# Attention's PSUM copies with the scheduler's rank of 60 instructions earlier

## The chip, the cores and the metric

One core of a Trainium2 chip runs the whole kernel. The metric is the device time of one execution in microseconds (us). The engines are named as in the profile: PE is TensorE (its matmuls; PEld its weight loads), DVE is VectorE, ACT is ScalarE, POOL is GpSimd, and SP is the queue that issues the DMAs. Matmuls write to PSUM, which has eight banks of 128 x 512 float32 words.

## The reference

One layer of a decoder trunk over 1024 tokens of width 1024: three token mixers side by side, a gated merge, an output projection and an MLP.

```
u = rms_norm(h, g_mix);  z = u @ w_in            # columns for all branches
y_nsa = nsa_mixer(q, k_c, v_c, k_s, v_s, k_w, v_w, gates)   # sparse attention
y_rnn = gelu(g_rnn) * rg_lru(causal_conv(x_rnn))            # recurrence
y_x   = cross_attention(q_x, mem) @ w_xo
h = h + (sum_b sigmoid(gate_b) * y_b) @ w_o
h = h + relu(rms_norm(h) @ w_up)**2 @ w_down;  out = rms_norm(h, g_final)
```

The sparse attention has 16 heads in 4 groups that share keys and values. For each block of 128 queries it adds three softmax attentions with their gates: over 63 compressed keys, over the 8 selected blocks of 64 keys (top-k of the compressed scores), and over a window of 512 keys.

## The kernel before

Every float32 product is made of float32r parts: an operand is split into a high part (a copy rounded by ACT) and a low part (the difference, by DVE), and `mm3` adds high x high, high x low and low x high in one PSUM bank. Transposed probabilities are split in the same way.

The program runs in stages. First the input is normalised and turned, the compressed keys and the first projections are made. Then comes the stage that matters here: cross attention and the sparse attention, with everything else that they don't need woven in between. After it come the output projection and the MLP.

Sparse attention walks over 4 groups g and 8 query blocks i, 32 units in all. `scores` makes the compressed scores, their softmax and, from the fifth block on, the top-k mask (`im`, `m`, `rp`, lines 741 to 760, on DVE and POOL). Then four pieces follow per unit (window and selected keys, two pairs of heads each). `sub_in` makes the scores of a piece in pss banks; the eviction at line 822 (DVE) adds the mask, writes E or Ew and takes the maximum; ACT makes the exponential (826); DVE and ACT scale by one over the sum and the gate (836 to 839). `sub_out` and `cmp_out` turn these probabilities: PE transposes four 128 x 128 blocks into a pst bank, `split_p` copies the bank to ph (ACT, 644) and the rest to pw (DVE, 645), and products with V add ph and pw into the unit's pso bank. `done` copies the finished pso to parts (ACT, 871) and stores it. PSUM has 2 banks for psg (projections), 2 for pst, 3 for pss and 1 for pso.

The woven work (`fill`) is a list of generators: projections of the groups, gates, the eight recurrences (`rnn_main`, r0 to r7) and merges. A `Weave` takes steps of `fill` so that they keep to 1.5 times PE's columns in attention. `rnn_main` has on ACT the Tanh and Exp of lines 938 to 940, Sqrt (944), Square (952) and on DVE the scan (951) and what follows.

What the program writes down is not the order in which engines run. Tile's scheduler goes over all instructions with a plan of its own of how long each takes, and whenever an engine is free in the plan it takes, among the instructions that are ready, that with the earliest rank; the rank is the place in the program. So the order on each engine is fixed when the program is built; on the chip each engine runs its list in that order, and semaphores hold what is not ready.

Of the kernel before, what the change touches and what calls it, by code (L numbers as in the profile page):

```python
# [12 lines left out]
AF = mybir.ActivationFunctionType  # L13
OP = mybir.AluOpType
# [32 lines left out]
HELD = 1  # L47
MIX = 1.5
LAG = 1


def seq(gens):
    for g in gens:
        yield from g
# [81 lines left out]
def body(tc, A, out):  # L136
    nc = tc.nc
    act, dve, pool, pe = nc.scalar, nc.vector, nc.gpsimd, TensorQueue(tc)
    dma = nc.sync.dma_start

    with ExitStack() as top:
# [97 lines left out]
        def load_split(src, shape, pl=w4, bufs=2, raw=None):  # L239
            if raw is None:  # L240
                raw = load_raw(src, shape, pl, bufs)
            hi = pl.tile(shape, F32R, name="whi", tag="whi", bufs=bufs)
            lo = pl.tile(shape, F32R, name="wlo", tag="wlo", bufs=bufs)
            if lo_engine[0] is pool and shape[1] == KC:
                act.activation(hi, raw, AF.Copy)  # L245
                for x in (slice(0, KC // 2), slice(KC // 2, KC)):
                    pool.tensor_tensor(lo[:, x], raw[:, x], hi[:, x], OP.subtract)  # L247
            else:
                split(hi, lo, raw, lo_eng=lo_engine[0])
            return hi, lo  # L250

        psum = top.enter_context(tc.tile_pool(name="psum", bufs=1, space=PSUM))
        with ExitStack() as mid:
# [50 lines left out]
            def z_weights(ci):  # L304
                return A["wz"][ci], [P, KC, P]
# [17 lines left out]
            with tc.tile_pool(name="e0", bufs=1) as e0:  # L323
# [55 lines left out]
                for ch in range(2):  # L379
                    zt = rw("zkv")  # L380
                    w = load_split(*z_weights(KV_CHUNK + 2 + ch))
# [259 lines left out]
            def split_p(pt, rows, w):  # L641
                ph = ap.tile([P, 512], F32R, name="ph", tag="ph", bufs=PB)
                pw = ap.tile([P, 512], F32R, name="pw", tag="pw", bufs=PB)
                act.activation(ph[:rows, :w], pt[:rows, :w], AF.Copy)  # L644
                dve.tensor_tensor(pw[:rows, :w], pt[:rows, :w], ph[:rows, :w], OP.subtract)  # L645
                return ph, pw

            def fold_out(po):
# [193 lines left out]
            def attention():  # L842
                queue = []

                def beside(a):
                    b = queue.pop(0) if len(queue) > LAG else iter(())
                    live = True
                    for _ in a:
                        yield
                        if live:  # L850
                            live = next(b, 0) is None
                            yield
                    for _ in b:
                        yield

                for g in range(G):
                    yield "wait", f"group{g}"
                    KV = [None, None]
                    for i in range(NQ):
                        nb, wb = i + 1, min(i + 1, 5)  # L860
                        ts = slice(i * P, (i + 1) * P)
                        q = load_q(q_hi[g, 0:4, :, ts].rearrange("h d t -> d h t"),
                                   q_lo[g, 0:4, :, ts].rearrange("h d t -> d h t"))
                        gts = gates[:, i, g * 12:(g + 1) * 12].rearrange("p (h b) -> p h b", b=3)
                        unit = {}
                        cS, sel_mask = scores(g, i, q, gts)
                        yield

                        def done(unit=unit, ts=ts, g=g):
                            t = ap.tile([P, 512], F32, name="parts", tag="fold", bufs=1)  # L870
                            act.activation(t, unit["po"], AF.Copy)
                            for y, part in zip(yn_d, (t[0:64], t[64:128])):
                                dma(y[2 * g:2 * g + 2].rearrange("c (e d) t -> d (c e) t", d=HD)[:, :, ts],
                                    part.rearrange("d (h q) -> d h q", q=P))
                        unit["done"] = done
                        for si, (br, p) in enumerate([(1, 0), (1, 1), (0, 0), (0, 1)]):
                            if i == 0 and p == 0:
                                KV[br] = load_kv(q_hi[g, 4 + br], q_lo[g, 4 + br], v_d[br, g], [P, S])
                            k0, n, mask = ((0, nb, sel_mask), (i + 1 - wb, wb, wmask[:, 640 - wb * P:]))[br]
                            Es = []  # L880
                            yield from beside(sub_in(Es, q, KV[br][:2], k0, n, mask, i, p, br, gts))
                            out_ = sub_out(unit, Es, KV[br][2], k0, n, p, si == 3)
                            queue.append(seq([cmp_out(unit, g, cS, 8 * nb), out_]) if si == 0 else out_)
                    if g:
                        yield "done", f"attn{g - 1}"
# [196 lines left out]
            def spare(name):  # L1082
                return fx.tile([P, 512], F32, name=name, tag="e", bufs=2)
# [185 lines left out]
            for j in range(NQ - 2):  # L1269
# [7 lines left out]
                if j == 0:  # L1277
                    for c in (6, 7):
                        t = spare("gm1")
# [8 lines left out]
            rows = [out_rows(NQ - 2)]  # L1288
# [122 lines left out]
            while n < len(dsteps):  # L1411
# [34 lines left out]
                for j in range(4):  # L1446
# [10 lines left out]
                    elif s == 2:  # L1457
                        t = h_half(j, 0)
                        dve.tensor_tensor(t, ps, t, OP.add)
                        dma(h_d[j][:, 0:512], t)  # L1460
                    elif s == 5:
                        v = keep_["v", j] = piece("dv")
                        dve.tensor_tensor(v, ps, keep_["u2", j], OP.add)
                        t = h_half(4 + j, 1)
                        pool.tensor_tensor(v, v, t, OP.add)
                        t = h_half(j, 1)
# [140 lines left out]
```

## Time and profile before

| | |
|---|---|
| median of 3 runs | 2135.46 us (2135.0 to 2138.74) |
| profiled execution | 2138.6 us |
| its span, first to last instruction | 2136.8 us |
| PE busy | 2000.6 us (94%) |
| DVE, ACT, POOL busy | 1463.2, 1135.0, 631.6 us |
| granted clock of PE, mean | 0.977 |

Busy time alone does not say what ends a stage. PE is the busiest engine throughout; where it stands idle, the row of its next instruction names what ended the wait. A granted clock of 1.00 is 2.4 GHz, 0.50 is 1.2 GHz.

### The profile page before, as it was taken

To read this page: it belongs to the slowest core of one execution; us is meant where nothing else is said; L and a number is where in the kernel's file an instruction comes from. 1 tells how busy PE (TensorE), PEld (TensorE's weight loads), DVE (VectorE), ACT (ScalarE), POOL (GpSimd) and SP (SyncE) were. 2 spreads that over 40 slices of the span, in tenths; PEclk is the share of its full clock that TensorE was granted. 3 is DMA by queue.
4 is the path that set the end of the run, shared out by engine and by line. 5 is a ranking of instruction groups with operands and counts; after the bars stand their busy time and mean duration, and the time that the engine had idled before them with its cause. 6 is when DMAs were issued, how large, how long until landed. Compare 5 with 4: busy or idle time off the path is not lost.

```text
span 2136.8 us, 30179 instructions
## 1 busy us (share of the span) xinstructions
PE 2000.6 (94%) x10276; PEld 1670.9 (78%) x10276; DVE 1463.2 (68%) x3211; ACT 1135.0 (53%) x2234; POOL 631.6 (30%) x573
## 2 busy tenths in 40 slices
PE   7988989999998999899999998999899999999997
PEld 6777868888877887777778787878688887888776
DVE  5344376776777777577877867855767777796564
ACT  5333367677667675585776756643322222444353
POOL 0010111242422433133432322311667774010210
PEclk9999999999999999999999999999999999999999
DMA  5655335311431212423123343453344446944433
GB/s 200 176 184 166 99 108 152 121 46 56 107 118 40 61 50 75 132 76 123 51 60 99 127 134 105 152 187 111 128 158 157 147 154 207 331 137 143 143 94 123
DMA packets 160578, 269.37 MB, mean 126 GB/s; under 512 B 19368, under 2 KB 71336, under 8 KB 160424
## 3 DMA queue, kind: packets, MB, share of 16 engines
q1 hardware_dynamic: 160424, 267.44, 40.5%
q8 instruction: 81, 1.33, 0.3%
q14 instruction: 73, 0.60, 0.1%
HBM read 180.87 MB, written 86.51 MB: 125 GB/s over the span
## 4 chain that ended last, share of the span: by engine, by line
PE 60%; DVE 15%; DMA 8%; ACT 6%; issue 6%; POOL 4%; SPq 1%; POOLq 0%; DVEq 0%; ACTq 0%
PE psg L80 29%; PE pss L80 16%; PE pst L80 6%; PE pso L80 5%; PE pst L84 4%; DVE pw L645 2%; DVE W L951 1%; DVE Ew L822 1%; DMA yn<-yn_d 1%; DMA q_hi<-W 1%; DMA wraw<-in_wz 1%; DVE sx L837 1%; DVE E L822 1%; DMA X<-kv_d 1%; DMA q_lo<-W 1%
## 5 line engine op out<-in xcount | busy, mean ns | idle before, releaser
L80 PE MATMUL psg<-uh,whi 128*128 128x512 f32 x928 | 383.3, 413 | 8.9 <-DVE qxl L225 6.2
L80 PE MATMUL psg<-uh,wlo 128*128 128x512 f32 x928 | 371.1, 400 | 0.5 <-DVE wlo L225 0.5
L80 PE MATMUL psg<-ul,whi 128*128 128x512 f32 x928 | 371.1, 400 | 0.0
L645 DVE TENSOR_TENSOR pw<-pst,ph 128x512 fp32r<-128x512 f32 (+1 forms) x352 | 217.4, 622 | 74.6 <-ACT ph L644 73.5
L644 ACT ACTIVATE ph<-pst 128x512 fp32r<-128x512 f32 (+1 forms) x352 | 187.3, 538 | 93.8 <-PE pst L84 92.5
L80 PEld LDWEIGHTS psg<-uh,wlo 128*128 128x128 f32 x928 | 177.8, 192 | 39.2 <-DVE wlo L225 0.9
L80 PEld LDWEIGHTS psg<-uh,whi 128*128 128x128 f32 x928 | 178.1, 192 | 37.2 <-DVE qxl L225 6.4
L80 PEld LDWEIGHTS psg<-ul,whi 128*128 128x128 f32 x928 | 178.4, 192 | 24.6 <-issue 0.4
L247 POOL TENSOR_TENSOR wlo<-wraw,whi 128x512 fp32r<-128x512 f32 x98 | 130.9, 1355 | 183.4 <-ACT whi L245 183.4
L80 PE MATMUL pss<-KA,Q 128*128 128x320 f32 (+5 forms) x416 | 145.0, 352 | 9.0 <-DVE sx L822 3.7
L80 PE MATMUL pso<-ph,V 128*128 128x256 f32 (+1 forms) x544 | 130.5, 305 | 8.1 <-DVE fold L652 6.1
L80 PE MATMUL pss<-KB,Q 128*128 128x320 f32 (+5 forms) x416 | 135.2, 329 | 0.0
L826 ACT ACTIVATE E<-E,sx 128x128 f32<-128x128 f32 (+7 forms) x128 | 98.8, 772 | 51.1 <-DVE sx L822 50.5
L80 PE MATMUL pso<-pw,V 128*128 128x256 f32 (+1 forms) x544 | 123.9, 294 | 0.0
L826 ACT ACTIVATE Ew<-Ew,sx 128x640 f32<-128x640 f32 (+4 forms) x128 | 88.5, 691 | 66.3 <-DVE sx L822 65.9
L84 PE MATMUL pst<-ident,E 128*128 128x128 f32 x576 | 95.3, 281 | 22.3 <-DVE pw L645 15.4
L80 PEld LDWEIGHTS pso<-ph,V 128*128 128x128 f32 x544 | 96.5, 193 | 23.0 <-DVE fold L652 6.4
L225 DVE TENSOR_TENSOR df<-araw,df 128x512 fp32r<-128x512 f32 x112 | 81.0, 728 | 47.7 <-ACT df L224 47.5
L80 PE MATMUL pss<-df 128*128 128x512 f32 x432 | 106.2, 389 | 0.7 <-ACT df L224 0.7
L224 ACT ACTIVATE df<-araw 128x512 fp32r<-128x512 f32 x112 | 69.1, 620 | 68.2 <-DMA araw<-act_d 29.3
L80 PE MATMUL psg<-df 128*128 128x512 f32 x384 | 99.0, 391 | 4.3 <-ACT df L224 3.2
L84 PEld LDWEIGHTS pst<-ident,E 128*128 128x128 f32 x576 | 71.9, 144 | 36.3 <-issue 21.6
(409 smaller groups left out, 5011.4 us busy)
## 6 DMA issues: line engine op xcount, KB each, us to landing
wraw<-in_wz SPq DMA_DIRECT2D x58, 512.0 KB
araw<-act_d SPq DMA_DIRECT2D x112, 256.0 KB
act_d<-as SPq DMA_DIRECT2D x64, 256.0 KB
act_d<-sq SPq DMA_DIRECT2D x48, 256.0 KB
yn_d<-parts SPq DMA_DIRECT2D x64, 128.0 KB
ura<-in_w_up SPq DMA_DIRECT2D x16, 512.0 KB
urb<-in_w_up SPq DMA_DIRECT2D x16, 512.0 KB
wdu<-in_w_down SPq DMA_DIRECT2D x32, 256.0 KB
```

Of the source, the lines that this page charges most:

```text
L80: self.tc.nc.tensor.matmul(out, w, x, start=start, stop=stop, skip_group_check=more)
L84: self.tc.nc.tensor.transpose(out, x, ident)
L224: act.activation(hi, src, AF.Copy)
L225: (lo_eng or dve).tensor_tensor(lo, src, hi, OP.subtract)
L247: pool.tensor_tensor(lo[:, x], raw[:, x], hi[:, x], OP.subtract)
L644: act.activation(ph[:rows, :w], pt[:rows, :w], AF.Copy)
L645: dve.tensor_tensor(pw[:rows, :w], pt[:rows, :w], ph[:rows, :w], OP.subtract)
L822: dve.tensor_tensor_reduce(E[:, c0:c0 + cw], ps[:, :cw], mask[:, c0:c0 + cw], -0.125, init, OP.add, OP.min, acc)
L826: act.activation(E[:, :nw], E[:, :nw], AF.Exp, bias=sx[:, hh:hh + 1], scale=-1.0, accum_out=sx[:, 2 + hh:3 + hh])
L837: dve.tensor_tensor(sx[:, 4:6], sx[:, 4:6], gts[:, 2 * p:2 * p + 2, 1 + br], OP.mult)
L951: dve.tensor_tensor_scan(gi[:, cs], r[:, cs], gi[:, cs], init, OP.mult, OP.add)
```

## The change

`tc.high_priority(60)` around an instruction gives it the rank of an instruction 60 places up in the program. The change puts it around ph and pw of `split_p` (cross attention's calls too) and around the copy to parts of `done`. Instructions, tiles and banks stay the same.

```diff
+AHEAD_OF_FILL = 60
...
             def split_p(pt, rows, w):
                 ph = ap.tile([P, 512], F32R, name="ph", tag="ph", bufs=PB)
                 pw = ap.tile([P, 512], F32R, name="pw", tag="pw", bufs=PB)
-                act.activation(ph[:rows, :w], pt[:rows, :w], AF.Copy)
-                dve.tensor_tensor(pw[:rows, :w], pt[:rows, :w], ph[:rows, :w], OP.subtract)
+                with tc.high_priority(AHEAD_OF_FILL):
+                    act.activation(ph[:rows, :w], pt[:rows, :w], AF.Copy)
+                    dve.tensor_tensor(pw[:rows, :w], pt[:rows, :w], ph[:rows, :w], OP.subtract)
                 return ph, pw
...
                             t = ap.tile([P, 512], F32, name="parts", tag="fold", bufs=1)
-                            act.activation(t, unit["po"], AF.Copy)
+                            with tc.high_priority(AHEAD_OF_FILL):
+                                act.activation(t, unit["po"], AF.Copy)
```

The order on the engines changes with it. The three pieces below are from one place, the first recurrence inside attention (about 445 to 460 us of the trace before). The numbers in the names tell tiles apart; lines of the changed program stand one to three further down (645 is 647, 822 is 824, 951 is 954).

DVE before: pst_4575 is the bank whose pw_4581 PE waits for, L951 the scan of the recurrence, L822 the score evictions (ISA; the second of each pair reads the minimum out).

```order
L822 ISA E_4570,sx_4569<-pss_4595,smask_4358,sx_4569 128x384
L822 ISA sx_4569 128x1
L645 TENSOR_TENSOR pw_4548<-pst_4544,ph_4547 128x256
L822 ISA E_4604,sx_4569<-pss_4605,smask_4358 128x384
L822 ISA sx_4569 128x1
L966 SCALAR_TENSOR_TENSOR gx_4412<-gx_4412,ysrc_4561 128x512
L822 ISA E_4604,sx_4569<-pss_4628,smask_4358,sx_4569 128x384
L822 ISA sx_4569 128x1
L951 SCALAR_TENSOR_TENSOR W3_3989<-W2_3988,W3_3989 128x512
L645 TENSOR_TENSOR pw_4581<-pst_4575,ph_4580 48x512
L953 TENSOR_SCALAR W1_3987<-W1_3987 128x512
L951 SCALAR_TENSOR_TENSOR W3_3989<-W2_3988,W3_3989 128x512
```

DVE after, around the same pw:

```order
L840 TENSOR_SCALAR Ew_4470<-Ew_4470,sx_4469 128x640
L647 TENSOR_TENSOR pw_4581<-pst_4575,ph_4580 48x512
L824 ISA E_4570,sx_4569<-pss_4595,smask_4358,sx_4569 128x384
L824 ISA sx_4569 128x1
L944 SCALAR_TENSOR_TENSOR tau_4537<-a2_4536,tau_4537 128x512
L824 ISA E_4604,sx_4569<-pss_4605,smask_4358 128x384
L824 ISA sx_4569 128x1
L969 SCALAR_TENSOR_TENSOR gx_4412<-gx_4412,ysrc_4561 128x512
L824 ISA E_4604,sx_4569<-pss_4628,smask_4358,sx_4569 128x384
L824 ISA sx_4569 128x1
L647 TENSOR_TENSOR pw_4625<-pst_4619,ph_4624 128x512
L954 SCALAR_TENSOR_TENSOR W3_3989<-W2_3988,W3_3989 128x512
```

pw_4581 stood behind the three evictions and the first scan; now it stands ahead of all of them. pw_4625, which stood two places behind the last row shown, is now ahead of both scans.

ACT before, in the same place: tau L944 are the Sqrt, W1 L952 a Square, E L826 exponentials.

```order
L944 ACTIVATE tau_4506<-tau_4506 128x512
L944 ACTIVATE tau_4537<-tau_4537 128x512
L644 ACTIVATE ph_4580<-pst_4575 48x512
L952 ACTIVATE W1_3987<-W0_3986 128x512
L826 ACT_TABLE_LOAD
L826 ACTIVATE E_4570,sx_4569<-E_4570,sx_4569 128x768
L952 ACTIVATE W1_3987<-W0_3986 128x512
L644 ACTIVATE ph_4624<-pst_4619 128x512
L826 ACTIVATE E_4604,sx_4569<-E_4604,sx_4569 128x768
```

ACT after:

```order
L646 ACTIVATE ph_4580<-pst_4575 48x512
L841 ACTIVATE Ew_4493<-Ew_4493,sx_4469 128x640
L942 ACTIVATE a2_4536<-W2_3988,cn2_574 128x512
L968 ACTIVATE gx_4412<-psg_4420 128x512
L943 ACTIVATE W2_3988<-W2_3988,cn_573 128x512
L947 ACT_TABLE_LOAD
L947 ACTIVATE tau_4506<-tau_4506 128x512
L646 ACTIVATE ph_4624<-pst_4619 128x512
L947 ACTIVATE tau_4537<-tau_4537 128x512
L955 ACTIVATE W1_3987<-W0_3986 128x512
L874 ACTIVATE parts_4648<-pso_4206 128x512
L646 ACTIVATE ph_4657<-pst_4652 128x512
```

ph_4580 stood behind both Sqrt and their table load and is now ahead of them; ph_4624 stood behind two Squares and an exponential, and is now between the Sqrt; the copy to parts of pso_4206 is ahead of the exponentials.

PE before, from the last product of the unit with bank pso_4206 on: pst_4652 are the next transposes, psg a projection of the woven work.

```order
L80 MATMUL pso_4206<-ph_4547,V_2973 128x256
L80 MATMUL pso_4206<-pw_4548,V_2973 128x256
L80 MATMUL psg_4584<-uh_99,whi_4190 128x512
L80 MATMUL psg_4584<-ul_101,whi_4190 128x512
L80 MATMUL psg_4584<-uh_99,wlo_4191 128x512
L84 MATMUL pst_4652<-ident_66,Ew_4362 128x128
L84 MATMUL pst_4652<-ident_66,Ew_4398 128x128
L84 MATMUL pst_4652<-ident_66,Ew_4362 128x128
L84 MATMUL pst_4652<-ident_66,Ew_4398 128x128
L80 MATMUL psg_4584<-uh_99,whi_4190 128x512
L80 MATMUL psg_4584<-ul_101,whi_4190 128x512
L80 MATMUL psg_4584<-uh_99,wlo_4191 128x512
```

PE after:

```order
L81 MATMUL pso_4206<-ph_4547,V_2973 128x256
L81 MATMUL pso_4206<-pw_4548,V_2973 128x256
L85 MATMUL pst_4652<-ident_66,Ew_4362 128x128
L85 MATMUL pst_4652<-ident_66,Ew_4398 128x128
L85 MATMUL pst_4652<-ident_66,Ew_4362 128x128
L85 MATMUL pst_4652<-ident_66,Ew_4398 128x128
L81 MATMUL psg_4584<-uh_99,whi_4190 128x512
L81 MATMUL psg_4584<-ul_101,whi_4190 128x512
L81 MATMUL psg_4584<-uh_99,wlo_4191 128x512
L81 MATMUL psg_4584<-uh_99,whi_4190 128x512
L81 MATMUL pso_4661<-ph_4580,VC_576 128x512
L81 MATMUL pso_4661<-pw_4581,VC_576 128x512
```

The transposes stand three products earlier, and the first products of the next unit, into pso_4661, follow the last of pso_4206 after four transposes and four projection products; before, they came only after 29 others.

## Rows read from the trace of the kernel before

**Rows 1.** The table of engines: busy time, share of the span, instructions.

```profile
PE 2000.6 (94%) x10276; PEld 1670.9 (78%) x10276; DVE 1463.2 (68%) x3211; ACT 1135.0 (53%) x2234; POOL 631.6 (30%) x573
```

**Rows 2.** Stretches: start:end, length, busy time by engine (instructions), PEclk, DMA share, GB/s.

```profile
295.00:1417.00 1122.00, 1048.98 (x5742) 880.68 (x5741) 822.85 (x2221) 740.08 (x1480) 351.94 (x380) 0.97 0.33 99
1417.00:2136.80 719.80, 691.92 (x3035) 567.19 (x3033) 494.05 (x691) 262.54 (x492) 250.99 (x164) 0.99 0.48 156
```

**Rows 3.** Waits of PE from 295 to 1417: us in total, times, longest us.

```profile
PE pst L84 <- DVE pw L645: 33.4, 26, 3.4
PE pso L80 <- ACT parts L871: 7.9, 6, 2.4
...
PE pst L84 <- DVE m L752: 5.6, 1, 5.6
PE pss L80 <- DVE sx L822: 3.7, 5, 1.5
...
PE pso L80 <- ACT ph L644: 2.0, 1, 2.0
```

**Rows 4.** Groups by line, 295 to 1417: busy us, mean ns; idle before, its releasers.

```profile
L645 DVE TENSOR_TENSOR pw<-pst,ph 128x512 fp32r<-128x512 f32 (+3 forms) x342 | 211.0, 620 | 74.3 <-ACT ph L644 73.2
L644 ACT ACTIVATE ph<-pst 128x512 fp32r<-128x512 f32 (+1 forms) x340 | 180.8, 536 | 93.1 <-PE pst L84 92.0 <-PE pso L80 0.2
...
L871 ACT ACTIVATE parts<-pso 128x512 f32<-128x512 f32 x32 | 18.7, 586 | 1.7 <-PE pso L80 1.7
```

**Rows 5.** Timeline of DVE near 454: start us, us, instruction, [idle before <-releaser].

```profile
451.86 2.28 DVE L951 TENSOR_TENSOR_SCAN W<-W,W 128x512 f32<-128x512 f32 x1 [0.84 <-POOL W L946]
454.06 0.66 DVE L645 TENSOR_TENSOR pw<-pst,ph 48x512 fp32r<-48x512 f32 x1
```

**Rows 6.** Timeline of ACT in the same place.

```profile
448.52 1.28 ACT L944 ACT_TABLE_LOAD   x1
449.82 1.16 ACT L944 ACTIVATE tau<-tau 128x512 f32<-128x512 f32 x2
450.88 0.57 ACT L644 ACTIVATE ph<-pst 48x512 fp32r<-48x512 f32 x1
```

**Rows 7.** Timeline of PE in the same place.

```profile
452.03 0.40 PE L80 MATMUL psg<-ul,whi 128*128 128x512 f32 x1
452.27 0.40 PE L80 MATMUL psg<-uh,wlo 128*128 128x512 f32 x1
454.87 1.09 PE L84 MATMUL pst<-ident,Ew 128*128 128x128 f32 x4 [2.20 <-DVE pw L645]
```

**Rows 8.** Timeline of DVE near 805.

```profile
803.82 1.27 DVE L749 SCALAR_TENSOR_TENSOR im<-hs,im 128x15 f32<-128x15 f32 x1
805.13 1.19 DVE L750 TENSOR_TENSOR im<-im,c_keep 128x16 f32<-128x16 f32 x1
...
807.47 0.68 DVE L645 TENSOR_TENSOR pw<-pst,ph 128x512 fp32r<-128x512 f32 x1
```

**Rows 9.** Timelines of PE near 808 and 874, and of ACT near 873.

```profile
808.30 0.41 PE L84 MATMUL pst<-ident,E 128*128 128x128 f32 x2 [3.39 <-DVE pw L645]
...
874.62 0.79 PE L80 MATMUL pso<-ph,VC 8*128 8x512 f32 x1 [2.39 <-ACT parts L871]
...
873.20 0.60 ACT L894 ACTIVATE W<-psg 128x512 f32<-128x512 f32 x1 [4.49 <-DMA q_hi<-W]
```

**Rows 10.** Stretches around two of the waits, columns as in rows 2.

```profile
454.80:458.20 3.40, 3.33 (x10) 2.88 (x11) 3.40 (x4) 2.28 (x6) 2.71 (x2) 0.50 0.00 0
458.20:461.60 3.40, 3.40 (x18) 2.68 (x17) 2.07 (x8) 1.44 (x3) 1.35 (x2) 1.00 0.32 77
...
1284.20:1291.00 6.80, 4.26 (x19) 4.24 (x20) 6.76 (x24) 3.64 (x7) 1.93 (x2) 0.50 0.31 97
```

**Rows 11.** A wait of DVE from 295 to 1417, and the stretch 1300 to 1375.

```profile
DVE pw L645 <- ACT ph L644: 73.2, 84, 4.7
...
1300.00:1375.00 75.00, 70.89 (x448) 61.63 (x446) 66.69 (x188) 56.58 (x102) 24.61 (x24) 0.95 0.35 107
```

## The prediction

> **What bounds the kernel now.** The table of engines comes first [rows 1]: PE is busy 94% of the span, DVE 68%, ACT 53%. So the time is PE's work plus what PE waits. The table of stretches says where a change to attention's copies can act [rows 2]: attention, with the other work woven into it, runs from about 295 to 1417 us. In those 1122.0 us PE is busy 1048.98, so it stands idle 73.0 us, and its mean granted clock is 0.97. Compared row by row, the two programs issue in the same order on PE before 295 us and behind 1417 us; only about 1,250 of PE's 10,276 instructions, all inside, have another place. I therefore leave the 295 us ahead and the 719.8 us behind as they are.
>
> The waits of PE in that stretch are next [rows 3]. 33.4 us in 26 waits end with a pw: the four transposes of a group want a pst bank, there are two, and the bank is free only when ACT has copied it (ph) and DVE has written the low part (pw). 7.9 us in 6 waits end with the copy of pso to parts (one bank), 2.0 us in 1 with a ph. One more, 5.6 us, is put down to a MAX8, but a pw ends just beside it and PE starts transposes: I count it as a pw wait. Together 48.9 us: the change can give back no more of PE's idle time than this. ph takes 0.54 us, pw 0.62, the copy to parts 0.59 [rows 4], so a bank could be empty some 1.2 us after its last transpose; longer is queueing.
>
> One such wait in full. At 454.87 PE starts transposes after 2.20 us of idleness [rows 7]. The pw it waited for ran at 454.06; ahead of it on DVE stood the scan of the recurrence (L951), for which DVE first sat idle 0.84 us (POOL) and which then took 2.28 us [rows 5]. The ph of that pw ended at 451.45, in that idle time, and had itself stood behind two Sqrt of the recurrence and their table load of 1.28 us [rows 6]. The same happens once in each of the eight recurrences (r0 to r7), at 454.9, 538.1, 694.2, 777.9, 937.5, 1025.4, 1109.5 and 1200.4 us, with 1.6 to 2.6 us of PE lost each time.
>
> **The change, part by part.** No instruction is added or taken away; ph, pw and parts get another rank, and the scheduler then orders all engines anew. On DVE 181 pw and on ACT 165 ph and 22 copies to parts now have an earlier place. The sum, against the span of 2136.8 us:
>
> *Eight recurrence waits.* In each the scan, and on ACT the Sqrt or the Square behind which the ph stood, are now behind (the order of the first is in the section on the change). What is left ahead of pw is its ph. I take the waits as gone: 8 x 2.1 us = -17 us. Bounds: 0 (another instruction takes the scan's place) to -18.
>
> *The other pw waits.* 39.0 - 17 = 22 us. I went through each in the timelines of ACT and DVE and took out what the new order puts behind. Where that is a scaling of E (L838), a gate product (L837) or a sum of the merge (L994), the wait goes: -9 us over some twenty waits, most under 1 us each. Where it is the top-k chain (L747 to L750), it stays: at 808.30 PE waited 3.39 us [rows 9] while pw stood behind rows of 1.27 and 1.19 us [rows 8], and these are still ahead of it. At the wait of 5.6 us part of the chain moves behind: -3. Together -12, bounds 0 to -22.
>
> *pso.* The one ph wait goes: -2. Of the copies to parts some move: -2 of 7.9. The largest, 2.39 us at 874.62, stays: the copy stands there behind ACT's L894, which had waited 4.49 us for a store [rows 9], and this row is still ahead. Bounds 0 to -10.
>
> *Clock.* After such a wait PE's clock can fall: in the 3.4 us behind the wait at 454.87 the granted clock is 0.50, the 1.2 GHz level, and 1.00 again in the next 3.4 [rows 10]; over 1284.2 to 1291.0 it is 0.50 as well, around the 5.6 us wait [rows 10]. A mean of 0.97 over the stretch [rows 2] is some 67 us at 0.50, in thirteen dips, six of them behind waits that I take as gone or halved. 3.4 us at half speed costs 1.7 us: six cost some 10. I take -6, since new waits will start dips of their own. Bounds +5 to -12.
>
> *Tighter packing, against the gain.* With its banks free earlier in its own plan, the scheduler pulls PE's next transposes and products forward. Walking PE's order and counting 0.23 us for a 512-column product (start to start, [rows 7]), 13 more bank reuses of pst (31, from 18 of 340) have under 2 us of PE work between the last transpose and the next. For pso it is 27 of 34, from 18: in seven units the cover was 2.9 to 7.2 us and is now 0.6 to 1.9 (the third piece of order shows one: four 512-column products and four transposes). A copy to parts costs 0.59 us plus what ACT is doing. In these seven, ACT still had 2 to 4 us ahead of it, so each can cost PE 0 to 3 us; I take 1.1: +8. For pst 13 x 0.25 = +3. Bounds 0 to +27.
>
> *What is pushed back.* The score evictions (L822) empty pss. 125 of 384 now stand behind one or two pw more, about 1 us. PE waits on them 3.7 us in 5 waits now [rows 3], and most have several us of slack. I take +6: bounds 0 to +20. It is likeliest between 1300 and 1375 us, where DVE is busy 66.69 of 75.00 us [rows 11]. The recurrence steps pushed back feed no PE instruction soon, and the stores of parts that move on SP do so by a few places, with the DMA engines at a share of 0.33 [rows 2]: nothing for either.
>
> Sum: -17 - 12 - 4 - 6 + 11 + 6 = **-22 us**, a span of 2114.8. The profiled execution took 2138.6, 1.8 more than its span and 3.1 more than the median of the runs, 2135.5. Since all the terms are differences, I take them off the median: **2113.5 us**.
>
> On a rule that speaks against the change: DVE sits idle 73.2 us in 84 waits at the head of its queue for a ph [rows 11], and in the 0.84 us before the scan [rows 5] it did not run a pw that was ready behind it. The Trainium skill (PSUM — Partial Sum Buffer, section "Engine vs sequencer instructions") says that the queues of ScalarE and VectorE are strict FIFO; the trace agrees with those 0.84 us. By that rule a pw raised to the head before its ph is done holds everything behind it, which is the second rival below; by it the sum would be that rival's +14.
>
> **The rivals.** *The waits come back (same).* The scheduler's plan fills the freed time by packing PE tighter, so pst and pso waits only change place. For it: the counts above, and that PE's waits of today already come from a plan that thought the bank free. Against it: in the recurrences the queueing of 3 us and more on DVE and ACT really leaves the path, and PE's order is unchanged or moved by a few products around half of them. Price: packing at its bound, +27, and the pushed-back work, +6, against -39: -6; with half of the -12 of the other waits not had either, 0. That is 2129 to 2136.
>
> *Blocked heads (slower).* A raised pw waits at the head of DVE for its ph, and the score evictions and scalings behind it go late; PE then waits for pss or for E. Place: 1300 to 1375, and each recurrence. Against it: DVE is idle 299 of the 1122 us [rows 2], and most evictions have slack. For it: 125 evictions moved. If one in three costs PE its 1 us, that is +42 in place of +6, so +14 in all: 2149.5 us. It decides from about 28 us of new PE waits on L822 and E.
>
> *More than forecast.* No new waits and the clock restored: -17 - 12 - 4 - 10 = -43, and up to -59 with all 48.9 us of [rows 3]: 2077 to 2098.
>
> *The rank does nothing.* Excluded, since the orders differ; it would be 2135.5.
>
> **How the numbers follow.** Forecast (2098 to 2128) 0.62; waits come back 0.17; slower 0.10; more than forecast 0.11. The range is 2093 to 2137: it leaves out the slower case and most of the best. About 0.2%, 4.3 us, is what a measurement of this kernel can tell from no change. Faster (under 2131.2): 0.62 + 0.11 and a small part of the second case, 0.76. Same: 0.14. Slower: 0.10.
>
> **What would show it.** Right: PE's waits for pw fall from 33.4 us to under 15, and none stands at a scan; the stretch from 295 takes about 1100 us in place of 1122; PE's work and both ends stay as they are. Tighter packing: PE's waits for parts stay near 8 us or grow to 15. Pushed back: PE's waits for L822 rise from 3.7 to some 10. The forecast is wrong if PE's idle time in the stretch is not under 65 us, or if waits on L822 or E take over the 33 us.

## The result and the profile after

The change makes the kernel a little slower: 2149.31 us in the median of 13 executions (2140.60 to 2157.14) against 2138.74 of 13 of the kernel before beside them, a ratio of 1.0055 with an interval of 1.0039 to 1.0070, some 11 us. The forecast was 2113.5 us, 22 us faster, with 2093 to 2137 as its range. A second set (run e15_change_again, the same program) gave 1.0065 (1.0046 to 1.0084).

The first profile fell on the slowest of the 13 executions (2157.14 us, span 2155.4). I therefore read it together with the profile of e15, whose span is 2145.3 us. The mean granted clock differs as well: 0.973 in the first profile, 0.979 in e15's, 0.977 in that of the kernel before. Over the 124 executions of the kernel before that were timed beside e1 to e17 (clock 0.974 to 0.980), an execution is on average about 1.1 us longer for each 0.001 of clock that it lacks. By this estimate e15's span is some 2 us shorter than it would be at 0.977, and the first profile's some 4 us longer. Busy time hardly moved from [rows 1]; this is the engine line of the first profile of after:

```profile
PE 2008.9 (93%) x10276; PEld 1680.0 (78%) x10276; DVE 1469.2 (68%) x3211; ACT 1136.1 (53%) x2234; POOL 638.3 (30%) x573
```

Where the time went is seen when the stretches are cut where PE issues the same instruction in both kernels. Below is the table of stretches of the kernel before, then of e15. The first three stretches are attention up to its last units, the fourth is the handover from attention's last products to the output projection, and what is left is the same work in both. First the limits and the length, then busy time per engine with counts, the clock, the DMA share.

```profile
294.50:1032.30 737.80, 689.51 (x3752) 577.61 (x3751) 534.51 (x1470) 491.50 (x998) 232.91 (x257) 0.97 0.30 89
1032.30:1222.00 189.70, 180.85 (x1001) 151.12 (x1000) 145.98 (x385) 134.93 (x273) 65.46 (x69) 0.99 0.29 86
1222.00:1358.30 136.30, 126.97 (x752) 109.15 (x751) 102.41 (x309) 84.48 (x161) 39.84 (x46) 0.97 0.36 113
1358.30:1429.20 70.90, 64.34 (x301) 53.17 (x300) 45.80 (x74) 33.18 (x63) 13.72 (x9) 0.90 0.63 204
```

```profile
295.50:1022.90 727.40, 683.97 (x3752) 574.59 (x3751) 533.16 (x1467) 490.62 (x999) 235.07 (x255) 0.98 0.31 91
1022.90:1220.40 197.50, 183.26 (x1001) 153.56 (x1000) 150.53 (x388) 136.30 (x272) 68.72 (x73) 0.97 0.28 82
1220.40:1356.80 136.40, 128.04 (x751) 110.09 (x750) 96.88 (x303) 81.35 (x157) 34.08 (x43) 0.97 0.34 105
1356.80:1439.00 82.20, 67.12 (x303) 55.38 (x302) 51.05 (x77) 36.59 (x68) 20.20 (x11) 0.90 0.59 189
```

The first 740 us gain 10.4 us (3.4 in the first profile of after), the next 190 lose 7.8, the third is unchanged: over the three, attention is 2.5 us shorter in e15 and 4.9 longer in the first profile of after. The handover then takes 82.2 us in place of 70.9, which is 11.3 us, about the whole loss. The first profile says the same (197.6 us for the second stretch, 83.3 for the handover).

The gain and the loss inside attention are in more than one profile. Cut at the same counts of PE instructions, the first stretch takes 724.9 to 734.4 us and the second 197.2 to 199.2 in the nine profiles of kernels that raise all three copies there by 60 (the two above, e1, e6, e9, e10, e13, e16, e17); in the four that keep the old order there (before, e2, e11, e12) they take 733.7 to 740.2 and 187.2 to 189.7. By the means, raised copies gain some 8 us in the first stretch and lose some 10 in the second.

Inside attention the eight waits at the recurrences are almost all gone. The waits of PE in the first profile of after, up to the handover (us in total, times, longest), answer to [rows 3]:

```profile
PE pst L85 <- DVE pw L647: 16.9, 13, 4.7
PE pso L81 <- ACT parts L874: 14.1, 7, 3.8
...
PE pss L81 <- DVE sx L824: 5.3, 6, 1.4
PE pst L85 <- DVE rp L755: 4.9, 1, 4.9
PE pst L85 <- POOL cS L738: 4.3, 5, 1.8
PE pst L85 <- DVE E L840: 3.6, 1, 3.6
```

Up to the handover the pw waits fell from 32.4 us (of the 33.4 in [rows 3]) to 16.9 (14.6 in e15), and of the eight waits at the recurrences, 16.4 us together, 0.4 us is left at the fourth (777.76 us, behind its second scan). At the first, DVE now runs the pw of 48 rows, which stood behind the scan [rows 5], 5.5 us ahead of it, and the next pw ahead of it too; PE shows no wait from 448 to 458 us:

```profile
447.41 0.68 DVE L647 TENSOR_TENSOR pw<-pst,ph 48x512 fp32r<-48x512 f32 x1
...
452.02 0.69 DVE L647 TENSOR_TENSOR pw<-pst,ph 128x512 fp32r<-128x512 f32 x1 [0.27 <-ACT ph L646]
452.92 2.30 DVE L954 TENSOR_TENSOR_SCAN W<-W,W 128x512 f32<-128x512 f32 x1 [0.20 <-POOL W L949]
```

But parts rose from 7.9 to 14.1 us, L824 from 3.7 to 5.3, and an E and more cS came in (the rp is a wait for a pw under another name, see the section on the prediction).

### The profile page after: what moved, and what is told of

The parts are those of the page before. It is cut to its first block, busy times and chain, and to the rows that moved or that the text cites. A ratio compares the mean times of both kernels' runs of the same rounds, so it can differ in the third digit from the quotient of the medians.

```text
span 2155.4 us, 30139 instructions
## 1 busy us (share of the span) xinstructions
PE 2008.9 (93%) x10276; PEld 1680.0 (78%) x10276; DVE 1469.2 (68%) x3211; ACT 1136.1 (53%) x2234; POOL 638.3 (30%) x573
## 5 line engine op out<-in xcount | busy, mean ns | idle before, releaser
L647 DVE TENSOR_TENSOR pw<-pst,ph 128x512 fp32r<-128x512 f32 (+1 forms) x352 | 217.3, 624 | 87.5 <-ACT ph L646 85.8
```

## Experiments: where the change costs

The working theory, A: the loss lies at the handover, and inside attention gain and loss cancel. Rival B: it is spread over attention, and the handover is chance. The copies are raised only up to the last two query blocks of the last group (e1, the diff below), or only in them (e2, the same with `>=`):

```diff
+            raised = [True]
...
+                with (tc.high_priority(AHEAD_OF_FILL) if raised[0] else nullcontext()):
...
+                        raised[0] = (g, i) < (G - 1, NQ - 2)
```

> ph, pw and parts keep their raised rank except in the last two query blocks of the last group, so the order of all engines at the handover from attention to the output projection is that of the kernel before. Theory A (the loss of 10.6 us lies at the handover: the profile of the changed kernel is 4.7 us late when attention ends and 17 to 21 us late just behind it): 2132 to 2141 us, and PE's waits between 295 and 1360 us as in the changed kernel. Theory B (the loss lies inside attention, by waits on parts and on pushed-back scalings): 2146 to 2152 us.

Measured: 1.0001 (0.9991 to 1.0012).

> The raised rank stands in the last two query blocks of the last group alone; the order before about 1310 us is that of the kernel before. Theory A: 2144 to 2152 us, with the loss behind 1360 us. Theory B: 2136 to 2140 us, the time of the kernel before.

Measured: 1.0044 (1.0028 to 1.0060). So nearly the whole loss comes from the copies of two of the 32 units, and raising all the others is worth nothing. The profiles agree: the handover takes 71.4 us in e1 and 79.7 in e2. A holds, B falls.

Next, which copies: only ph and pw, or only the copy to parts.

> Only ph and pw are raised, the copy to parts has its old rank. Theory C (the raised copy to parts is what costs: it pulls the next unit's first products on PE and the stores on SP forward, and the merges' loads stand behind these stores): 2120 to 2135 us, PE's waits on parts at 8 us or less, SP's waits for parts near 35 us in place of 54. Theory D (what costs is ph and pw pushing score evictions and scalings back): 2145 to 2152 us.

Measured: 1.0036 (1.0021 to 1.0050), a median of 2143.65 us, which lies between the two expectations and nearer to D's.

> Only the copy to parts is raised. Theory C: 2145 to 2152 us, the eight waits behind the recurrences' scans still there and PE's waits on parts over 12 us. Theory D: 2134 to 2139 us.

Measured: 1.0006 (0.9992 to 1.0019). It is ph and pw that cost; raising parts alone is neutral, as D said. Where the 7 us of e3 go is open: in its one profile the handover takes only 72.6 us.

## Experiments: why attention gains nothing

Theory F: the eight scan waits were worth their 17 us, and the new order of PE that raised copies bring gave it back. Rival G: a cure of the scan waits is used up by the next thing that is late. The test cures the scan waits without raising a copy:

```diff
+BEHIND = 60
...
+                        with tc.high_priority(-BEHIND):
                             act.activation(tau, tau, AF.Sqrt)
...
+                        with tc.high_priority(-BEHIND):
                             dve.tensor_tensor_scan(gi[:, cs], r[:, cs], ...)
                             act.activation(t[:, cs], gr[:, cs], AF.Square)
```

> No copy is raised; instead the recurrence's two Sqrt, two scans and two Squares get the rank of an instruction 60 places down. The pw that stood behind a scan is now ahead of it in all eight recurrences, as with the change, but only some 360 PE instructions have another place (with the copies raised in the same part: 990). Theory F (the eight scan waits were worth their 17 us; what gave it back in attention was the new order of PE that raised copies bring, with its waits on parts, E and L822): ratio 0.992 to 0.996, and waits on parts stay near 8 us. Rival G (any cure of the scan waits is used up by the next thing that is late, since DVE and ACT have the same work to do in the same time): ratio 0.998 to 1.002, the scan waits gone and other waits grown by about as much.

Measured: 1.0043 (1.0028 to 1.0057): F falls, and the kernel is even slower than G said. Of the 16.4 us that PE waited for a pw at the scans 5.4 are left, in five waits for a pw that has a scan among the six DVE instructions ahead of it (0.4 us in one with the change). Yet PE's waits up to the handover are longer than before:

```profile
PE pst L85 <- DVE pw L646: 34.0, 24, 5.4
PE pso L81 <- ACT parts L872: 13.5, 8, 2.9
PE pss L81 <- DVE sx L823: 5.8, 6, 1.5
```

Before, the same three rows were 32.4, 7.9 and 3.7 us. The kernel's loss is here: attention's three stretches take 1074.1 us against 1063.8, the handover 70.5 against 70.9. Where one wait went is seen 17 us behind the first recurrence. First DVE, then PE, of the same run:

```profile
469.87 0.69 DVE L961 SCALAR_TENSOR_TENSOR W<-W,W 128x512 f32<-128x512 f32 x1 [3.94 <-ACT W L960]
470.48 0.68 DVE L646 TENSOR_TENSOR pw<-pst,ph 128x512 fp32r<-128x512 f32 x1
```

```profile
471.22 1.06 PE L85 MATMUL pst<-ident,E 128*128 128x128 f32 x4 [3.29 <-DVE pw L646]
```

The later step of the same recurrence (L961, which needs ACT's Tanh of L960, itself later now) sits at the head of DVE's queue for 3.94 us, and a pw stands behind it. Before, PE lost nothing there. In this one place the recurrence was moved and took its wait along.

With the copies raised, the 17 us go another way. The stretch from 1022.9 us, in which e15 loses 7.8 us, is as long in every kernel that raises all three copies there (see above). Its two largest waits, ACT and PE first, then DVE and PE (e15):

```profile
1112.69 1.15 ACT L828 ACTIVATE E<-E,sx 128x1024 f32<-128x1024 f32 x1 [0.89 <-DVE sx L824]
...
1113.84 0.58 ACT L874 ACTIVATE parts<-pso 128x512 f32<-128x512 f32 x1
```

```profile
1114.46 0.51 PE L81 MATMUL pso<-ph,VC 64*128 64x512 f32 x1 [3.82 <-ACT parts L874]
```

```profile
1206.53 1.23 DVE L839 TENSOR_TENSOR sx<-sx,gates 128x2 f32<-128x2 f32 x1
1207.68 0.41 DVE L647 TENSOR_TENSOR pw<-pst,ph 128x256 fp32r<-128x256 f32 x1
1208.01 0.41 DVE L840 TENSOR_SCALAR E<-E,sx 128x384 f32<-128x384 f32 x1
```

```profile
1208.57 1.08 PE L85 MATMUL pst<-ident,E 128*128 128x128 f32 x4 [3.60 <-DVE E L840]
```

In the first, the copy to parts stands on ACT behind an exponential that waits for an eviction, and PE, pulled forward, has no products left to cover it. In the second, the scaling of E that PE needs comes behind two raised pw (0.68 us at 1205.57 and 0.41 at 1207.68) and a gate product of 1.23 us between them, whose median is 0.16 in 128. What may have made it long is in the last section.

Two more offsets and parts of the change:

> The change with 200 places in place of 60. Inside attention it raises more; at the handover its order differs (late gate products woven in from 54 products earlier, 24 products ahead of the first row's transposes, the merges' loads ahead of the last stores of parts). Theory A2: no loss at the handover, ratio 0.997 to 1.003. Rival H: the copies are raised all the more, ratio 1.004 or above. If waits inside attention grow with the offset, the pw waits fall below 22 us and those on parts, E and L822 rise above 26 us.

Measured: 1.0039 (1.0026 to 1.0051); pw waits fell further, to 14.6 us up to the handover, but parts stand at 14.2 and cS and E at 7.2 and 4.6. In its profile attention's three stretches take 1061.9 us, against 1063.8 before, and the handover 76.3: the ratio is outside A2's range (A2 is put to the test below) and just under what its rival H named.

> Only ph (ACT) is raised by 60, pw and parts keep their rank. The handover is nearly as before (12 products ahead of the first row's transposes). Theory I (inside attention raised pw block DVE's queue while they wait for ph): DVE's idle time for ph, 73 us before and 86 with the change, stays at 73 or falls, and the ratio is 0.995 to 0.999. Rival F/G (it is PE's repacking): parts waits grow to 12 us or more, ratio 0.999 to 1.003.

Measured: 1.0022 (1.0009 to 1.0034). With pw at its old rank nothing is gained either, and parts take 18.5 us, as the rival said. But DVE's idle time for ph did not go back to 73 us: it is 80.9. So what that idle time costs is not tested by this run. (The edit is the `with` around ph alone.)

## Experiments: what costs at the handover

In e15 PE waits at the handover are these, and before (1358.3 to 1429.2 us) those below:

```profile
PE pss L85 <- DVE xres L1134: 5.1, 1, 5.1
PE pst L85 <- DVE pw L647: 4.8, 2, 2.8
PE psg L81 <- ACT gm L1060: 4.3, 1, 4.3
```

```profile
PE pss L84 <- DVE xres L1131: 2.5, 1, 2.5
PE pso L80 <- ACT ph L644: 2.0, 1, 2.0
PE psg L80 <- ACT yh L224: 1.2, 2, 1.0
PE pst L84 <- DVE pw L645: 0.9, 1, 0.9
```

A2 looked at PE: the late gate products were no longer woven among the last transposes.

```diff
+LATE = 200
...
+                    with tc.high_priority(LATE):
                         for _ in z_half(late[c - 6], hf, use):
                             pass
```

> The change in full, and besides the late gate products (the eight half gates behind attention) get the rank of an instruction 200 places up. They are then woven among attention's last transposes again, until behind the last product of attention, and 24 products of the second output row stand ahead of the first row's transposes (6 with the change alone, 12 before). Theory A2 (the loss at the handover is that PE has no other work while the last pst banks are emptied, and starts the first output row's transposes too early): most of the 9 us come back, ratio 0.997 to 1.002. Rival H (the loss at the handover is on DVE, ACT and SP, where raised copies push the merges and the splits of the output rows behind): ratio stays 1.003 to 1.006.

Measured: 1.0050 (1.0035 to 1.0066). With PE's order mended nothing came back (the handover takes 79.1 us); the wait stands in one piece ahead of the first row's products:

```profile
PE psg L82 <- ACT yh L226: 11.4, 1, 11.4
```

A2 falls, and what is late is what the row needs.

That is a chain over DRAM: a unit's parts are stored, the merge loads them (L993 to L996, L1048 to L1050), DVE merges, the result is stored and loaded as a row of y (yr, L1111), split into yh and yl, and multiplied. All these transfers go through SP's one queue. SP in e15, then before (only rows on one merge, on the copies, and on a late merge's load):

```profile
1350.06 1.25 SPq L876 DMA_DIRECT2D yn_d<-parts  x2
1351.41 0.55 SPq L993 DMA_DIRECT2D yn<-yn_d  x1
1360.42 0.33 SPq L1048 DMA_DIRECT2D ymerge<-yn_d  x1
...
1365.80 0.38 SPq L994 DMA_DIRECT2D yn<-yn_d  x1
1366.22 0.43 SPq L995 DMA_DIRECT2D tn<-tn_d  x1
```

```profile
1348.77 0.32 SPq L990 DMA_DIRECT2D yn<-yn_d  x1
1351.21 0.32 SPq L992 DMA_DIRECT2D tn<-tn_d  x1
...
1353.19 0.43 SPq L991 DMA_DIRECT2D yn<-yn_d  x1
1353.71 1.24 SPq L873 DMA_DIRECT2D yn_d<-parts  x2
```

The same three loads of one merge are done at 1353 us before and at 1366 in e15: the store of parts stands ahead of them now, and a load of the late merge (L1048), also ahead of two of them, waits for PE. These are the two largest rows of SP's waits in e15 from 1320 to 1430 us:

```profile
SPq L876 <- ACT parts L874: 32.7, 2, 20.0
SPq L1048 <- PE pso L81: 8.4, 1, 8.4
```

e2 shows that this is not the whole: there the three loads are done at 1351 us, ahead of attention's end as before, and the handover still takes 79.7 us. What e15 and e2 share are late loads of the rows: the second row's last load (yr) is issued 48 us behind the end of attention before, 61 in e15 and 55 in e2. That is no proof, since these loads also wait for what comes ahead of them.

In e15 the merge stands on DVE among the raised pw of the last transposes. DVE and PE in e15 (gm itself had waited 2.99 us for a load of ymerge):

```profile
1369.65 1.20 DVE L997 TENSOR_TENSOR yn<-yn,yn 128x512 f32<-128x512 f32 x1
1370.88 2.74 DVE L998 SCALAR_TENSOR_TENSOR yn<-tn,yn 128x512 f32<-128x512 f32 x1
1373.55 1.27 DVE L647 TENSOR_TENSOR pw<-pst,ph 128x512 fp32r<-128x512 f32 x2
```

```profile
1374.28 0.83 PE L85 MATMUL pst<-ident,E 128*128 128x128 f32 x4 [2.01 <-DVE pw L647]
1382.88 0.79 PE L81 MATMUL psg<-uh,whi 128*128 128x512 f32 x1 [4.27 <-ACT gm L1060]
```

Theory J: SP's order is the cause. Rival K: the raised copies on DVE and ACT, and SP's order only goes with them. Each edit gives another rank or queue to DMA issues alone, but the scheduler orders all engines anew, so some instructions of PE, DVE and ACT near the handover get another place too. Three edits, singly and together: the loads of y for the first two rows get an earlier rank; the last unit's stores of parts a later one; or the stores of the last two units are issued by ACT.

```diff
+ROWS = 300
...
+                    with tc.high_priority(ROWS if j < 2 else 0):
                         dma(yr, y_d[j // 4]...)
```

```diff
+                                put = nc.scalar.dma_start if g == G - 1 and ts.start >= (NQ - 2) * P else dma
-                                dma(y[2 * g:2 * g + 2]...
+                                put(y[2 * g:2 * g + 2]...
```

> The change in full, and besides the loads of y for the first two output rows (yr) get the rank of an instruction 300 places up. On SP the second row's four loads then stand ahead of the loads of the late merges (590 to 597; with the change alone 592, 603, 605, 607, behind those loads and a store that waits for DVE's merge), and 24 products of the second row stand ahead of the first row's transposes (6). Theory J (part of the loss at the handover is SP's order: the row loads stand behind others that wait): the 5.3 us wait at the first row's transposes goes, some 4 to 6 us of the 10 come back, ratio 1.001 to 1.003. Rival K (DVE and ACT, where the raised copies push the merges and the row splits back, and SP's order is only its companion): ratio stays 1.004 to 1.006.

Measured: 1.0040 (1.0026 to 1.0053). That is outside J's range, at the lower end of K's. Still the wait at the first row's transposes is gone from the profile, the handover takes 76.0 us against 82.2, and some 3 to 5 us came back by the ratios; the gm and pw waits stay (5.3 and 4.6 us). PE's order changed with the loads (24 products of the second row ahead of the transposes); e6 had such an order without the loads and gained nothing.

> As the run with the row loads raised, and besides the two stores of the last unit's parts get the rank of an instruction 100 places down, so that on SP they stand behind the loads of the first late merges (580 against 574; with the change alone they stand ahead, 575 against 578, and SP waited 20.4 us there for the copy to parts). Theory J: both blocks on SP gone, ratio 0.998 to 1.001. Rival K: 1.004 to 1.006.

Measured: 1.0024 (1.0012 to 1.0037), more than half of the loss back, between both expectations. The 20 us wait that the expectation names is not at these stores: in e15 it is at the last unit's but one (1350.06 us). The edit moved that place too: in e10 the three loads of the merge are done at 1358 us, ahead of the late merge's load.

> Copies raised only in the last two query blocks (alone that took 1.0044), and the loads of y for the first two output rows raised by 300. On SP the last stores of parts stand behind the merges' loads in this kernel anyway, as before the change; what the raised copies alone moved there is the second row's loads (602 to 607 against 592 to 606), and they now stand at 592 to 598. The wait of 7.6 us at the first row's transposes should go. Theory J: ratio 0.998 to 1.001. Rival K: 1.003 to 1.005.

Measured: 1.0017 (1.0003 to 1.0032) against 1.0044 without the row loads: some 6 us back with the order of a few loads on SP, between both expectations. PE's wait of 7.4 us at the first row's transposes (e2: 1406.72 us, put down to yh) is gone. The gain stands in the medians alone: e11's profile fell on its slowest execution (2151.24 us), and there the handover still takes 79.2 us, with 3.8 us for a pw and 3.0 for yh in place of that wait.

> No copy raised, only the loads of y for the first two output rows by 300. Before, PE waits 2.6 us at the first row's transposes and 1.4 us for the second row's yh (1407 and 1410 us of the trace before). Theory J: both shrink, and this kernel is the fastest of the four: ratio 0.997 to 0.999. Rival K, or that the freed 4 us are waited for behind it (the late merges' loads are now later): 0.999 to 1.002.

Measured: 0.9988 (0.9976 to 0.9999). Without any raised copy the row loads gain about 2.5 us, the fastest kernel here, at the edge of what can be told apart: its executions also had a clock of 0.978 in the mean against 0.977 beside them. Of PE's waits at the first two rows 0.7 us is left, and 2.6 us come back as a wait of the third row, whose loads stand behind now.

> The change in full, but the four stores of parts of the last two units are issued by ACT, behind its own copy, and not by SP. PE's order is that of the change but for 115 to 120 of its 10,276 instructions, and the raised copies stand as with the change. Theory J (a store of parts stands ahead of the merges' loads on SP and holds them for 20 us; late merges then stand ahead of pw on DVE at attention's last transposes): that block is gone, the pw and gm waits at the handover (9 us in the second profile of the change) fall to 3 or less, ratio 1.0005 to 1.0035 (the row loads are still as with the change). Rival K (the raised copies on DVE and ACT do it): ratio 1.004 to 1.0065.

Measured: 1.0020 (1.0007 to 1.0032), some 7 to 10 us better than the change (1.0055 and 1.0065), with every copy still raised: in J's range and outside K's. By the traces of e15 and e16, 31 of DVE's 3211 and 12 of ACT's 2234 instructions have another place too, so it is the edit of the four stores that is shown to give this back, not each step behind it.

> The same, and the loads of y of the first two output rows raised by 300: neither a store of the last two units nor the late merges' loads stand ahead of what the handover needs on SP. Theory J: 0.998 to 1.001, the whole loss of the change gone with every copy still raised. Rival K: 1.003 to 1.005.

Measured: 1.0014 (1.0002 to 1.0027). The handover takes 74.7 us in e16 and 74.5 in e17, against 82.2 in e15 and 70.9 before. This is between both expectations and nearer to J's. So edits of SP's queue take back most of the loss. They don't take back all: against e12, which has the row loads alone (0.9988), e17 is still some 5 to 6 us slower. What I had written of J's inside was partly wrong: the pw and gm waits should have fallen to 3 us or less together; in e16 they are 4.5 and 2.8, and e17 still has

```profile
PE pso L82 <- DVE pw L648: 4.3, 2, 4.1
PE psg L82 <- ACT gm L1062: 2.8, 1, 2.8
```

And the 20 us for which SP waited at the store of parts are not the price: before, SP waits 16.6 us in the same place, for the buffer of the merge's own load (freed by rp), in e16 19.5 us for the same, and it gets on at almost the same time (1348.77 before, 1350.06 in e15). Nor is it shown which load costs. In e16 the late merge's load still stands ahead of two of the three loads and waits 9.3 us for PE, and they are done at 1364 us, 2 to 3 us earlier than in e15, while the second row's last load is issued 53 us behind attention's end, 8 earlier than in e15. No run separates the two. What is left in e17 may be K's; no run separates that either.

Last, whether attention's gain was only hidden by the handover. Both kernels raise everywhere but in the last two blocks and have the row loads of e12:

> Copies raised by 60 everywhere except in the last two query blocks, and the loads of y for the first two output rows raised by 300. If what attention gains and loses inside itself cancels, as the run without the row loads showed (1.0001), this equals the kernel that has the row loads alone (0.9988): 0.998 to 1.000. If part of a gain in attention was hidden by the handover, it is under 0.9975.

Measured: 1.0003 (0.9991 to 1.0015), a little above the first expectation.

> As the run before, with 200 places in place of 60. In the profile of the change with 200 places attention was 13 us ahead of the kernel before at 1030 us and 7 ahead at 1320. If that gain is in the orders and not in the single execution, the ratio is 0.994 to 0.997, and this beats all others. If the waits only change place (parts, cS and E in place of pw), it is 0.998 to 1.001.

Measured: 1.0005 (0.9994 to 1.0016). There is no hidden gain: against the kernel before, raised copies inside attention are neutral at 60 and at 200 places. Against e12, which has the row loads without them, both are some 3 us slower, which the intervals don't tell from nothing.

> The changed kernel itself once more, for a second profile: the first fell on its slowest execution (2157.1 us, 7.8 above its median). Expected: median 2147 to 2151; between the last products of attention and the second output row PE loses 8 to 13 us against the kernel before, with the wait of SP at the store of parts and the one at the first row's transposes there again; inside attention within 5 us of the kernel before.

Measured: median 2152.35 us, 1.4 above the expected range, ratio 1.0065. In attention e15 ends 1.5 us ahead of before, and the handover costs 11.3 us, with SP's wait (20.0 us) and the one at the first row's transposes (5.1), as expected. No version beats the kernel before by more than the 2.5 us of e12.

## Why the prediction was wrong, step by step

**Eight recurrence waits, -17.** Right in itself: of their 16.4 us 0.4 is left. The pw waits up to the handover fell by 15.5 us (17.8 in e15). Two of the long waits change names between the profiles, so they have to be counted in: that of 5.6 us at 1286.74, put down to m, is 4.4 us and put down to pw now, and that of 3.39 us at 808.30, which was to stay, grew to 4.9 and is put down to rp. With them the fall is 16 to 18.5 us.

**The other pw waits, -12.** Wrong: hardly anything beyond the recurrences came. I followed each wait against the new order as if nothing else would take its place. One wait of e5 shows how that fails: the wait for a late step moves to the next pw that stands behind it.

**pso and tighter packing, -4 + 11.** Right for pso: -2 and +8 came to +6, and parts rose by 6.2 us (7.9 to 14.1). The +3 for pst can't be told from the rest of the pw waits.

**What is pushed back, +6.** L822 cost 1.6 more, not 6. But I had priced only the evictions, and nothing for what else goes behind a raised copy. The scaling of E, which I had counted as moving out of pw's way, cost 3.6 us in one wait, and cS, W, xE and sx some 5 more in small ones.

**Clock, -6.** Not had. The mean clock is 0.97 or 0.98 in the first stretch before and after, and falls from 0.99 to 0.97 in the second: the new waits bring their own dips. From 295 to 1417 us the clock is at 0.50 for 65 us in 13 dips before, for 68 us in 12 in the first profile of after, and for 61 us in 13 in e15.

So attention's sum was -16 to -18.5 for pw, +6 for parts, +2 for L822, +9 for E, cS and the like, with the clock about even: within a few us of nothing, where I had -22. PE's idle time says the same: over the three stretches it is 66.5 us before, 68.8 in the first profile of after and 66.0 in e15. That is the first rival, "the waits come back", at about its price.

**Stores of parts that move on SP, "nothing".** The step that decides the sign, and it failed. Both ends did stay as they are: from the instruction that PE issues at 1418.8 us before, the rest takes 718.0 us before and 717.2 in e15. The loss lies in the 60 us ahead of it (60.5 against 71.3 us), inside the stretch of the forecast, where the last parts pass through DRAM to the output rows. The sentence that let it go was "the stores of parts that move on SP do so by a few places ...: nothing", and the sum has no term for the loads that move with them. e11 and e16 price such places at some 6 and 7 to 10 us. The mean DMA share of 0.33 on which I rested it says how busy the DMA engines were; it does not say whether a queue in order holds a load that somebody needs. At the handover the share is 0.63 before and 0.59 in e15.

**The second rival, slower,** named nearly the measured time (2149.5), by a mechanism that did not happen: it wanted 28 us of new waits on L822 and E, and there were 5. DVE's idle time at a pw for its ph did grow, from [rows 11] 73.2 us to 85.8; what it cost is open, since it is 80.9 in e8. The row that was to show such a blocked head is weaker than I wrote: the ph ended at 451.45 us [rows 6], so the pw was ready for 0.41 of the 0.84 us ahead of the scan.

## What to carry to other kernels

A scheduler's rank moves everything: before it is given to a copy in a loop, look at where the loop ends, and at the stores and loads that become ready earlier in the plan and so stand in another order on the DMA queue. Where every engine has work, waits can queue up again at the next head; price a removed wait by what is late next, or take it at zero. A last iteration whose results the next stage waits for should keep its order: in e1 leaving out 2 blocks of 32 undid the whole loss.

## What the runs showed of the hardware

The same DVE instruction takes 0.68 us or four times that. L998 on 128 x 512 took 2.74 us at 1370.88 in e15 against a median of 0.685 in 12; its longest row before was 0.693. POOL ran three long subtractions beside it, here on POOL in e15:

```profile
1367.93 7.92 POOL L226 TENSOR_TENSOR wol<-woraw,woh 128x1024 fp32r<-128x1024 f32 x3 [2.58 <-ACT woh L225]
```

The Trainium skill (SBUF — State Buffer, section "SBUF: two separate sides") says that DVE and GpSimd share one pair of ports as an exclusive lock, which a DVE operation with two SBUF inputs and a GpSimd operation that reads SBUF hold for a whole instruction. The rows fit that: 0.68 us and up to one 2.6 us POOL subtraction (7.92 us for three). The gate product of 1.23 us at 1206.53, a DVE operation with two SBUF inputs as well, fits it too: it ended at 1207.76 us, and beside it POOL ran two subtractions that ended at 1207.75.

```profile
1205.25 2.50 POOL L248 TENSOR_TENSOR wlo<-wraw,whi 128x512 fp32r<-128x512 f32 x2
```

No run took POOL's work away, so the cause of the long rows is read, not tested. They made DVE later just where a pw, and the scaling of E, stood behind them.
